# Scoring 64 expert blocks and gathering 36 rows while the PEER gates are laid out

## The chip, the core and the metric

One core of a Trainium2 chip runs the whole program. The metric is device time in microseconds from the first to the last instruction's end. The engines are TensorE (PE, with its weight loads as PEld), VectorE (DVE), ScalarE (ACT), GpSimd (POOL) and SyncE (SP), which here only issues DMAs.

## What is computed

The reference runs two transformer blocks on 512 tokens of width 1024. The change lies in the first block's PEER layer:

```
q      = (hf @ w_query).reshape(t, 8, 256)
s1, s2 = q halves against peer_keys1, peer_keys2         # 128 scores each
v1, i1 = top_k(s1, 16);  v2, i2 = top_k(s2, 16)
sc, ci = top_k(v1[..., :, None] + v2[..., None, :], 16)  # 16 of 256 pairs
idx    = i1 * 128 + i2 of the chosen pairs;  gates = softmax(sc)
a      = gelu(hf . peer_u[idx]);  out = sum(gates * a * peer_v[idx])
```

Each token chooses 8 x 16 = 128 of 16384 experts.

## The kernel before

The 512 tokens are four blocks of 128. Blocks 0 to 2 (384 tokens, `NDT = 3`) are computed **densely**: all 16384 experts, in 128 expert blocks of 128, are scored against them by matrix products, weighted by a gate tensor that is zero where an expert was not chosen, and multiplied by `peer_v`. Block 3 is computed by **gathering**: for each of its 128 choices per token, one indirect DMA fetches a row of `peer_u` (later of `peer_v`) for each of 128 tokens, 512 KB in all.

The float32 products are made of three float32r products (`mm3`): an operand is split into a high part (ACT copies it, `act(hi, raw, AF.Copy)`) and a low part (raw minus high, a TENSOR_TENSOR, L439 for `peer_u`).

The stages of `peer`, in the order of the program:

- `queries(h)` for eight heads: query products, keys, top 16.
- `decode(0)`: a generator that turns block 0's top 16s into expert numbers and gates. It has ten yields. After each one, `early_u(1)` scores one expert block ahead of its turn: load (`uraw`, four buffers), high part (ACT, L438), low part (DVE, L439), 24 matmuls (`aps`, two PSUM buffers), Gelu (ACT, L622), store to DRAM (`Ad`, SP, L623). Which blocks are scored early is set by `AHEAD`: 5 of every 16, that is 40 of 128 (`EARLY`). The tiles `uhi` and `ulo` have two buffers each.
- `spread(t, step)` for t = 0, 1, 2: lays the gates of token block t out as a dense tensor. It has 8 steps, so 24 in all. A step makes one-hot tiles `of` (16 TENSOR_SCALAR, DVE, L601) and `ob` (2, DVE, L605), widens `ob` to `oq` (2, ACT, L606), multiplies them (`gps`, PE, L610), copies the product out (4, ACT, L612) and stores it (2 DMAs on SP, L614). After each step, `step()` runs `early_u(1)` and two yields of `decode(t + 1)`. `decode(3)` ends with `gidx`, the row numbers for the gathers, and `ggate`.
- `early_u(len(EARLY))`: the six early blocks that are left.
- The main loop over the 128 expert blocks, in an order written out by hand (`manual_schedule`): a block that was not scored early is scored (24 matmuls with 384 columns), then weighted, split and multiplied by `peer_v` (18 matmuls with 512 columns into six PSUM accumulators). `pace` puts `gather_step(n)` between them, n = 0 to 255: an indirect DMA (POOL, L652) and its use, for n below 128 a multiply with row sum (L659), then a multiply-add into `gacc` (L665). `row` has five buffers here.

Outside `manual_schedule` the order of each engine's instructions is chosen by the framework's scheduler, which may take an instruction of a later step first when its inputs are ready; each engine then runs its own list strictly in order. The second block of the reference follows and is not touched.

Of the kernel before, what the change touches and what calls it, by code (L numbers as in the profile page):

```python
# [9 lines left out]
F32 = mybir.dt.float32  # L10
# [4 lines left out]
AF = mybir.ActivationFunctionType  # L15
ALU = mybir.AluOpType
# [4 lines left out]
P = 128  # L21
D = 1024
# [3 lines left out]
NEG = -1e30  # L26
LOW = -3e38
NDT = 3
TD = NDT * P
AHEAD = (1, 4, 7, 10, 13)  # L30
MAGIC = 12582912.0
TWO_PI_HI = 6.28125
TWO_PI_LO = 2.0 * math.pi - 6.28125
# [2 lines left out]
def body(ctx, tc, I, O):  # L36
# [355 lines left out]
    with ExitStack() as px:  # L392
        peer(px, tc, I, locals())
# [9 lines left out]
def peer(px, tc, I, E):  # L403
    nc = tc.nc
    mm = nc.tensor.matmul
    act = nc.scalar.activation
    vtt = nc.vector.tensor_tensor
    vts = nc.vector.tensor_scalar
    stt = nc.vector.scalar_tensor_tensor
# [9 lines left out]
    htm = kp.tile([P, D], F32, name="htm", tag="htm")  # L419
    gidx = kp.tile([P, P], I32, name="gidx", tag="gidx")  # L420
    ggate = kp.tile([P, P], F32, name="ggate", tag="ggate")
    e1T = kp.tile([P, TD], F32, name="e1T", tag="e1T")
    e2T = kp.tile([P, TD], BF16, name="e2T", tag="e2T")
    gT = kp.tile([P, TD], F32, name="gT", tag="gT")
    gs2 = kp.tile([P, KD], F32, name="gs2", tag="gs2")
    NBK = TD // 16
    Gd = [drp.tile([P, NBK, 64, 16], F32, name=f"Gd{c}") for c in range(2)]
    up = E["up"]
    papp = px.enter_context(tc.tile_pool(name="papp", bufs=2, space=PSUM))
    EARLY = [e for e in range(P) if e % 16 in AHEAD]  # L430
    Ad = drp.tile([len(EARLY), P, TD], F32, name="Ad")

    def u_split(e, lo_engine):
        raw = up.tile([P, KD, P], F32, name="uraw", tag="uraw", bufs=4)
        nc.sync.dma_start(raw, I["peer_uT"][e])
        hi = up.tile([P, KD, P], F32R, name="uhi", tag="uhi")
        lo = up.tile([P, KD, P], F32R, name="ulo", tag="ulo")
        act(hi, raw, AF.Copy)  # L438
        lo_engine.tensor_tensor(lo, raw, hi.bitcast(F32), op=ALU.subtract)  # L439
        return hi, lo  # L440

    def u_matmuls(hi, lo):
        ps = papp.tile([P, TD], F32, name="aps", tag="aps")
        for k in range(KD):
            mm3(ps, hi[:, k], lo[:, k], hh[:, k, :TD], hl[:, k, :TD], k == 0, k == KD - 1)
        return ps

    with ExitStack() as qx:
        gp = qx.enter_context(tc.tile_pool(name="gp", bufs=2))
        ioj = gp.tile([P, 16, P], BF16, name="ioj", tag="ioj", bufs=1)  # L450
# [45 lines left out]
        def queries(h):  # L496
            qT = []
            for half in range(2):
                if h == 0:
                    ps = ps0[half]  # L500
                else:
                    ps = pp.tile([P, T], F32, name="mmp", tag="mmp")
                    proj_block(ps, wq.get(2 * h + half), (hh, hl))
                q = qp.tile([P, T], F32, name="qT", tag="qT", bufs=4)
                act(q, ps, AF.Copy)
                qT.append(q)
            for t in (3, 0, 1, 2):
                sp = pp.tile([P, 2, P], F32, name="sp", tag="sp", bufs=2)
                for half in range(2):
                    mm(sp[:, half], qT[half][:, t * P:(t + 1) * P], keysT[:, 2 * h + half], start=True, stop=True)  # L510
                s = sq_.tile([P, 2, P], F32, name="s", tag="s", bufs=4)
                act(s, sp, AF.Copy)
                for half in range(2):
                    top16(VVs[:, t, h, half], IIs[:, t, h, half], s[:, half])
# [79 lines left out]
        def spread(t, step):  # L594
            for blk in range(8 * t, 8 * t + 8):
                st = gp.tile([P, P, 16], F32, name="st", tag="st")
                for hb in range(2):
                    c0 = 16 * blk + 8 * hb
                    of = gp.tile([P, 8, P], F32, name="of", tag="of")
                    for j in range(8):  # L600
                        vts(of[:, j], iop, e1T[:, c0 + j:c0 + j + 1], gT[:, c0 + j:c0 + j + 1],  # L601
                            op0=ALU.is_equal, op1=ALU.mult)
                    oq = gp.tile([P, 8, P], F32, name="oq", tag="oq")
                    ob2 = gp.tile([P, P, 8], BF16, name="ob2", tag="ob2")
                    vtt(ob2, iob, e2T[:, None, c0:c0 + 8].to_broadcast([P, P, 8]), op=ALU.is_equal)  # L605
                    act(oq.rearrange("p t e -> p e t"), ob2, AF.Copy)  # L606
                    for t4 in range(2):
                        ps = pp.tile([P, 4, P], F32, name="gps", tag="gps")
                        for j in range(4):
                            mm(ps[:, j], oq[:, 4 * t4 + j], of[:, 4 * t4 + j], start=True, stop=True)  # L610
                        o = 8 * hb + 4 * t4
                        act(st[:, :, o:o + 4], ps.rearrange("p t e -> p e t"), AF.Copy)  # L612
                for c in range(2):
                    nc.sync.dma_start(Gd[c][:, blk], st[:, 64 * c:64 * c + 64])  # L614
                step()

        early = iter(range(len(EARLY)))

        def early_u(count):
            for n in itertools.islice(early, count):  # L620
                gl = up.tile([P, TD], F32, name="gle", tag="gle", bufs=2)
                act(gl, u_matmuls(*u_split(EARLY[n], nc.vector)), AF.Gelu)  # L622
                nc.sync.dma_start(Ad[n], gl)  # L623

        for h in range(8):
            queries(h)
        for _ in decode(0):
            early_u(1)
        for t in range(NDT):
            dec = decode(t + 1)  # L630

            def step():
                early_u(1)
                for _ in itertools.islice(dec, 2):
                    pass

            spread(t, step)
            for _ in dec:
                pass

    early_u(len(EARLY))


    rp = px.enter_context(tc.tile_pool(name="rp", bufs=1))
    outp = rp.tile([P, D], F32, name="gacc", tag="gacc")
    nc.vector.memset(outp, 0.0)
    ga = rp.tile([P, P], F32, name="ga", tag="ga")
    scr = rp.tile([P, D], F32, name="gscr", tag="gscr")

    def gather(src, j):  # L650
        row = rp.tile([P, D], F32, name="row", tag="row", bufs=5)
        nc.gpsimd.indirect_dma_start(out=row, out_offset=None, in_=I[src],  # L652
                                     in_offset=bass.IndirectOffsetOnAxis(ap=gidx[:, j:j + 1], axis=0))
        return row

    def gather_step(n):
        if n < P:
            row = gather("peer_u", n)
            stt(scr, row, 1.0, htm, op0=ALU.mult, op1=ALU.mult, accum_out=ga[:, n:n + 1])  # L659
        else:  # L660
            if n == P:
                act(ga, ga, AF.Gelu)
                vtt(ga, ga, ggate, op=ALU.mult)
            row = gather("peer_v", n - P)
            stt(outp, row, ga[:, n - P:n - P + 1], outp, op0=ALU.mult, op1=ALU.add)  # L665

    ppo = px.enter_context(tc.tile_pool(name="ppo", bufs=1, space=PSUM))
    acc = [[ppo.tile([P, T], F32, name=f"acc{t}{c}", tag=f"acc{t}{c}") for c in range(2)] for t in range(NDT)]
    GG = 8
# [33 lines left out]
    def v_matmuls(e, wh, wl, vh, vl):  # L703
        order = [(t, c) for t in range(NDT) for c in range(2)]
        if e == P - 1:
            order.sort(key=lambda tc_: tc_[1])
        for t, c in order:
            mm3(acc[t][c], wh[:, t * P:(t + 1) * P], wl[:, t * P:(t + 1) * P],
                vh[:, c * T:(c + 1) * T], vl[:, c * T:(c + 1) * T], e == 0, e == P - 1)

    total = 2 * P - len(EARLY) - 4
    done = [0, 0]

    def pace(units):
        done[0] += units
        while done[1] < 2 * P and done[1] * total < done[0] * 2 * P:
            gather_step(done[1])
            done[1] += 1

# [47 lines left out]
    for c in range(2):  # L767
        sts = [rp.tile([P, T], F32, name="ot", tag="row", bufs=5) for t in range(NDT)]
        for t in range(NDT):
            act(sts[t], acc[t][c], AF.Copy)  # L770
# [769 lines left out]
```

## Time and profile before

| | us |
|---|---|
| median of 3 runs (2838.25 to 2846.59) | 2843.0 |
| the profiled execution | 2841.45 |
| its span, first to last instruction | 2839.7 |
| PE busy (12617 matmuls) | 2586.8 (91%) |
| DVE busy | 1445.1 (51%) |
| ACT busy | 915.6 (32%) |
| POOL busy | 451.3 (16%) |

The shares are over the whole span; the stages differ greatly, and the argument is read by stage. A busy time counts overlapping instructions once. Matmuls are pipelined, so one that "lasts" 0.34 us starts about 0.17 us after the one before it: the cost of a run of matmuls is read from their starts.

### The profile page before, as it was taken

How to read it: one execution, taken by the hardware profiler on the slowest of the kernel's cores; microseconds unless marked ns; L12 is line 12 of the kernel's file. 1: busy time of each engine (PE TensorE's matmuls, PEld its weight loads, DVE VectorE, ACT ScalarE, POOL GpSimd, SP SyncE). 2: the span in 40 equal slices, each digit the busy share in tenths (PEclk: the TensorE clock that was granted, in tenths of full speed). 3: DMA queues.
4: the chain of work that ended last, by engine and by line, in shares of the span. 5: the costliest groups of instructions: out<-in, count | busy, mean ns of one | idle time of the engine just before them, and what ended most of it. 6: DMA issues, size and time to landing. Idle time of an engine off the chain costs nothing. (4 is left out here: it accounts for less than half of the span.)

```text
span 2839.7 us, 32851 instructions
## 1 busy us (share of the span) xinstructions
PE 2586.8 (91%) x12617; PEld 1810.0 (64%) x12617; DVE 1445.1 (51%) x2879; ACT 915.6 (32%) x1369; POOL 451.3 (16%) x335
## 2 busy tenths in 40 slices
PE   7998999988999999999999999969888888788887
PEld 5666778988899889988898777633323223232332
DVE  4485899994777877778777655330101101011011
ACT  4463438984333333333333434220000000000001
POOL 0001000000444444344444113010000000000000
PEclk9999999999999999999999999989999999999999
DMA  6344224556889899889988422379999999999997
GB/s 237 121 160 163 75 93 175 212 193 223 306 314 330 310 316 331 317 308 319 321 311 318 155 93 79 123 302 428 428 427 426 429 427 428 428 428 428 427 428 305
DMA packets 195078, 826.41 MB, mean 291 GB/s; under 512 B 17160, under 2 KB 77448, under 8 KB 167145
## 3 DMA queue, kind: packets, MB, share of 16 engines
q1 hardware_dynamic: 154280, 680.67, 61.1%
q0 software_dynamic: 38016, 138.43, 13.7%
q10 hardware_dynamic: 2624, 5.22, 0.5%
q8 instruction: 99, 1.62, 0.2%
q14 instruction: 59, 0.48, 0.1%
HBM read 787.02 MB, written 37.22 MB: 290 GB/s over the span
## 5 line engine op out<-in xcount | busy, mean ns | idle before, releaser
L1349 DVE TENSOR_TENSOR sg<-sg,upp 128x512 f32<-128x512 f32 x32 | 22.0, 688 | 754.7 <-PE upp L1342 754.7
L85 PE MATMUL aps<-hh,uhi 128*128 128x384 f32 x1024 | 348.3, 340 | 7.9 <-ACT gle L622 7.9
L87 PE MATMUL aps<-hh,ulo 128*128 128x384 f32 x1024 | 346.1, 338 | 5.1 <-DVE ulo L439 5.1
L86 PE MATMUL aps<-hl,uhi 128*128 128x384 f32 x1024 | 345.9, 338 | 0.0
L1342 PE MATMUL upp<-wch,XB 128*64 128x512 f32 x1024 | 269.1, 616 | 46.2 <-DMA wch<-in_w_up 46.2
L1342 PE MATMUL gp<-wch,XB 128*64 128x512 f32 x1024 | 273.1, 620 | 37.5 <-DMA wch<-in_w_gate 37.5
L85 PE MATMUL acc<-vh,wh 128*128 128x512 f32 x768 | 300.0, 391 | 2.4 <-ACT wh L81 2.4
L87 PE MATMUL acc<-vh,wl 128*128 128x512 f32 x768 | 300.4, 391 | 0.0
L86 PE MATMUL acc<-vl,wh 128*128 128x512 f32 x768 | 299.9, 390 | 0.3 <-DVE vl L82 0.3
L652 POOL DMA_INDIRECT row<-in_peer_u,gidx x128 | 191.3, 1494 | 633.9 <-issue 386.9
L1368 PE MATMUL y<-wch,aT 128*64 128x512 f32 x1024 | 247.6, 598 | 11.9 <-ACT aT L1354 11.9
L652 POOL DMA_INDIRECT row<-in_peer_v,gidx x128 | 187.1, 1462 | 254.2 <-DVE gacc L665 221.5
L1342 PEld LDWEIGHTS gp<-wch,XB 128*64 128x64 f32 x1024 | 85.3, 142 | 206.3 <-issue 149.4
L1342 PEld LDWEIGHTS upp<-wch,XB 128*64 128x64 f32 x1024 | 84.8, 141 | 204.0 <-issue 138.2
L438 ACT ACTIVATE uhi<-uraw 128x1024 fp32r<-128x1024 f32 x128 | 135.6, 1059 | 235.1 <-DMA uraw<-in_peer_uT 185.0
L439 DVE TENSOR_TENSOR ulo<-uraw,uhi 128x1024 fp32r<-128x1024 f32 x128 | 156.4, 1222 | 106.4 <-ACT uhi L438 105.6
L85 PEld LDWEIGHTS aps<-hh,uhi 128*128 128x128 f32 x1024 | 194.2, 190 | 13.0 <-ACT gle L622 9.5
L87 PEld LDWEIGHTS aps<-hh,ulo 128*128 128x128 f32 x1024 | 193.8, 189 | 6.1 <-DVE ulo L439 6.1
L86 PEld LDWEIGHTS aps<-hl,uhi 128*128 128x128 f32 x1024 | 194.2, 190 | 4.0
L1348 ACT ACTIVATE sg<-gp 128x512 f32<-128x512 f32 x32 | 19.1, 597 | 491.7 <-PE gp L1342 491.7
L1368 PEld LDWEIGHTS y<-wch,aT 128*64 128x64 f32 x1024 | 84.9, 136 | 141.4 <-issue 122.6
L665 DVE SCALAR_TENSOR_TENSOR gacc<-row,ga,gacc 128x1024 f32<-128x1024 f32 x128 | 164.1, 1282 | 2.4
(406 smaller groups left out, 4261.5 us busy)
## 6 DMA issues: line engine op xcount, KB each, us to landing
wch<-in_w_gate SPq DMA_DIRECT2D x64, 2048.0 KB, 35.4
wch<-in_w_up SPq DMA_DIRECT2D x62, 2048.0 KB, 33.0
wch<-in_w_down SPq DMA_DIRECT2D x62, 2048.0 KB, 34.4
uraw<-in_peer_uT SPq DMA_DIRECT2D x128, 512.0 KB, 7.7
vraw<-in_peer_v SPq DMA_DIRECT2D x128, 512.0 KB, 6.6
Gd<-st SPq DMA_DIRECT2D x48, 512.0 KB, 3.6
gg<-Gd SPq DMA_DIRECT2D x16, 1536.0 KB, 16.5
wraw<-in_w_in SPq DMA_DIRECT2D x36, 512.0 KB, 3.2
```

The lines of the kernel that those rows point to most:

```text
L85: mm(out, lh, rh, start=first, stop=False)
L86: mm(out, lh, rl, start=False, stop=False)
L87: mm(out, ll, rh, start=False, stop=last)
L438: act(hi, raw, AF.Copy)
L439: lo_engine.tensor_tensor(lo, raw, hi.bitcast(F32), op=ALU.subtract)
L652: nc.gpsimd.indirect_dma_start(out=row, out_offset=None, in_=I[src], in_offset=bass.IndirectOffsetOnAxis(ap=gidx[:, j:j + 1], axis=0))
L665: stt(outp, row, ga[:, n - P:n - P + 1], outp, op0=ALU.mult, op1=ALU.add)
L1342: mm(ps[64 * e:64 * e + 64], xT[:, k, 64 * e:64 * e + 64], gu[w][e][:, o:o + T], start=k == 0, stop=k == KD - 1)
L1348: act(sg, ps2[0], AF.Silu)
L1349: vtt(sg, sg, ps2[1], op=ALU.mult)
L1368: mm(y[c][64 * e:64 * e + 64], aT[:, fb, 64 * e:64 * e + 64], dn[e][:, o:o + T], start=fc == 0 and fb == 0, stop=fc == 3 and fb == 3)
```

## The change

`AHEAD` names 8 of every 16 blocks in place of 5 (the odd ones), so 64 blocks are scored early. In `decode(0)`'s early blocks, the low part is made on GpSimd. In `spread`, each step scores two blocks in place of one. The decodes of the other three token blocks run in the order 1, 3, 2 in one chain of yields. From the step in which `decode(3)` has ended (the eleventh of 24), each step also uses the two rows gathered one step before and gathers two more, into a pool `gr` with two buffers of its own; after the last step, five rounds of one early block and one such `rows_step` bring the number of rows to `NGE = 36`. One early block is left for the end. The use of a `peer_u` row now writes its product over the row in place of a scratch tile. The main loop starts its gathers at row 36 and spreads the remaining 220 over its length.

```diff
-AHEAD = (1, 4, 7, 10, 13)
+NGE = 36
+AHEAD = (1, 3, 5, 7, 9, 11, 13, 15)
...
+    gr = px.enter_context(tc.tile_pool(name="gr", bufs=1))
+    ga = gr.tile([P, P], F32, name="ga", tag="ga")
+    sums, homes = [], [(gr, 2)]
+
+    def gather(n):
+        pool, bufs = homes[-1]
+        row = pool.tile([P, D], F32, name="row", tag="row", bufs=bufs)
+        j = n % P
+        nc.gpsimd.indirect_dma_start(out=row, out_offset=None, in_=I["peer_u" if n < P else "peer_v"],
+                                     in_offset=bass.IndirectOffsetOnAxis(ap=gidx[:, j:j + 1], axis=0))
+        return row
+
+    def use_row(n, row):
+        if n < P:
+            stt(row, row, 1.0, htm, op0=ALU.mult, op1=ALU.mult, accum_out=ga[:, n:n + 1])
+        else:
...
+    def gather_step(n):
+        use_row(n, gather(n))
...
-        def early_u(count):
+        def early_u(count, sub=nc.vector):
...
-                act(gl, u_matmuls(*u_split(EARLY[n], nc.vector)), AF.Gelu)
+                act(gl, u_matmuls(*u_split(EARLY[n], sub)), AF.Gelu)
...
         for _ in decode(0):
+            early_u(1, nc.gpsimd)
+        ended = []
+
+        def decodes():
+            for t in (1, 3, 2):
+                yield from decode(t)
+                ended.append(t)
+
+        dec = decodes()
+        rows = []
+
+        def rows_step():
+            for n, row in rows:
+                use_row(n, row)
+            n0 = rows[-1][0] + 1 if rows else 0
+            rows[:] = [(n, gather(n)) for n in range(n0, min(n0 + 2, NGE))]
+
+        def step():
+            early_u(2)
+            for _ in itertools.islice(dec, 2):
+                pass
+            if 3 in ended and (not rows or rows[-1][0] + 1 < NGE):
+                rows_step()
+
+        for t in range(NDT):
+            while t and t not in ended:
+                next(dec, None)
+            spread(t, step)
+        while rows:
             early_u(1)
-        for t in range(NDT):
-            dec = decode(t + 1)
-
-            def step():
-                early_u(1)
-                for _ in itertools.islice(dec, 2):
-                    pass
-
-            spread(t, step)
-            for _ in dec:
-                pass
+            rows_step()
...
-    ga = rp.tile([P, P], F32, name="ga", tag="ga")
-    scr = rp.tile([P, D], F32, name="gscr", tag="gscr")
...
+    sums.append(outp)
+    homes.append((rp, 5))
...
-    done = [0, 0]
+    done = [0, NGE]
...
-        while done[1] < 2 * P and done[1] * total < done[0] * 2 * P:
+        while done[1] < 2 * P and (done[1] - NGE) * total < done[0] * (2 * P - NGE):
```

## Rows read from the trace of the kernel before

**Rows 1.** Busy time in four stretches: start:end, length, PE, PEld, DVE, ACT, POOL.

```profile
408.40:452.00 43.60, 36.31 (x195) 34.92 (x196) 42.26 (x193) 24.86 (x29) 0.00 (x0) 0.96 0.38 134
452.00:664.00 212.00, 192.92 (x1326) 184.85 (x1327) 194.37 (x656) 185.99 (x207) 0.00 (x0) 0.98 0.53 196
664.00:705.00 41.00, 35.31 (x193) 34.36 (x191) 11.51 (x11) 13.48 (x19) 5.14 (x5) 0.95 0.72 260
705.00:1580.00 875.00, 874.51 (x4330) 784.12 (x4331) 689.05 (x849) 319.52 (x425) 373.24 (x251) 1.00 0.90 315
```

**Rows 2.** PE's timeline in the main loop: start, us, engine, line, operation.

```profile
1002.67 0.34 PE L85 MATMUL aps<-hh,uhi 128*128 128x384 f32 x1
...
1006.83 0.39 PE L85 MATMUL acc<-vh,wh 128*128 128x512 f32 x1
...
1015.00 0.34 PE L85 MATMUL aps<-hh,uhi 128*128 128x384 f32 x1
```

**Rows 3.** PE's costliest group from 452 to 664 us.

```profile
L610 PE MATMUL gps<-of,oq 128*128 128x128 f32 x768 | 98.3, 282 | 17.7 <-ACT oq L606 9.8 <-ACT st L612 7.9
```

**Rows 4.** PE's waits from 408.4 to 452 us: total us, times, longest.

```profile
PE aps L87 <- DVE ulo L439: 5.1, 3, 2.0
PE aps L85 <- ACT gle L622: 2.2, 2, 1.3
```

**Rows 5.** PE's two largest waits from 452 to 664 us.

```profile
PE gps L610 <- ACT oq L606: 9.8, 10, 1.5
PE gps L610 <- ACT st L612: 7.9, 9, 1.6
```

**Rows 6.** Waits from 664 to 705 us.

```profile
ACT gle L622 <- DMA Ad<-gle: 6.4, 2, 6.1
...
PE aps L85 <- ACT gle L622: 3.4, 1, 3.4
```

**Rows 7.** DVE's costliest groups from 452 to 664 us.

```profile
L601 DVE TENSOR_SCALAR of<-iop,e1T,gT 128x128 f32<-128x128 f32 x384 | 103.8, 344 | 10.5 <-PE gps L610 10.3
L605 DVE TENSOR_TENSOR ob<-iob,e2T 128x1024 bf16<-128x1024 bf16 x48 | 32.5, 687 | 2.9 <-ACT oq L606 2.9
L439 DVE TENSOR_TENSOR ulo<-uraw,uhi 128x1024 fp32r<-128x1024 f32 x24 | 29.3, 1221 | 1.9 <-ACT uhi L438 1.8
```

**Rows 8.** ACT's groups from 452 to 664 us.

```profile
L606 ACT ACTIVATE oq<-ob 128x1024 f32<-128x1024 bf16 x48 | 98.1, 2052 | 8.4 <-DVE ob L605 8.4
...
L438 ACT ACTIVATE uhi<-uraw 128x1024 fp32r<-128x1024 f32 x24 | 25.5, 1061 | 8.6 <-PE aps L86 8.6
L622 ACT ACTIVATE gle<-aps 128x384 f32<-128x384 f32 x23 | 11.1, 483 | 0.0
```

**Rows 9.** The use of a `peer_u` row on DVE, whole span.

```profile
L659 DVE SCALAR_TENSOR_TENSOR gscr<-row,htm 128x1024 f32<-128x1024 f32 x128 | 156.4, 1222 | 2.3
...
L659 DVE DVE_READ_ACCUMULATOR gscr<-row,htm 128x1 f32 x128 | 10.6, 83 | 0.0
```

**Rows 10.** A TENSOR_TENSOR of 128x1024 on POOL, by form.

```profile
L478 POOL TENSOR_TENSOR hg<-hh,hl 128x1024 f32<-128x1024 f32 x1 | 2.4, 2389 | 23.1 <-DVE hl L169 23.1
```

**Rows 11.** DVE's timeline, 243 to 272 us.

```profile
243.11 1.21 DVE L219 SCALAR_TENSOR_TENSOR wada<-wada,c 128x1024 f32<-128x1024 f32 x1
...
244.25 2.30 DVE L219 SCALAR_TENSOR_TENSOR wada<-wada,c 128x1024 f32<-128x1024 f32 x1
```

**Rows 12.** POOL's timeline in the same stretch.

```profile
244.01 1.47 POOL L386 TENSOR_TENSOR sx<-sx,sq 128x512 f32<-128x512 f32 x1 [1.36 <-ACT sq L133]
```

**Rows 13.** POOL's timeline, 660 to 760 us: two gathers of the first five.

```profile
671.16 1.12 POOL L652 DMA_INDIRECT row<-in_peer_u,gidx  x1 [366.79 <-issue]
672.59 0.93 POOL L652 DMA_INDIRECT row<-in_peer_u,gidx  x1 [0.30 <-issue]
```

**Rows 14.** DMA issue to landing of all 256 gathers, by source line.

```profile
DMA to landing us min/median/max: 4.9/8.0/11.2
```

**Rows 15.** The same of the five gathers issued from 660 to 680 us.

```profile
DMA to landing us min/median/max: 9.4/9.8/10.1
```

**Rows 16.** ACT's timeline, 380 to 460 us: decode(1)'s widening and the first `oq`.

```profile
442.31 1.91 ACT L560 ACTIVATE wb__3862<-d 128x2048 bf16<-128x2048 f32 x1
...
455.59 2.07 ACT L606 ACTIVATE oq<-ob 128x1024 f32<-128x1024 bf16 x1 [3.38 <-DVE ob L605]
```

**Rows 17.** DMA traffic from 705 to 1580 us.

```profile
DMA packets 118808, 275.30 MB, mean 315 GB/s; under 512 B 8288, under 2 KB 59360, under 8 KB 118752
```

More of the change, by code (lines that the diff above doesn't have):

```diff
@@ L446, in u_matmuls @@
         return ps
+    gr = px.enter_context(tc.tile_pool(name="gr", bufs=1))
[12 more added lines that the diff above has]
+        else:
+            if n == P:
+                act(ga, ga, AF.Gelu)
+                vtt(ga, ga, ggate, op=ALU.mult)
+            stt(sums[0], row, ga[:, n - P:n - P + 1], sums[0], op0=ALU.mult, op1=ALU.add)
+    def gather_step(n):
+        use_row(n, gather(n))
     with ExitStack() as qx:
@@ L646, in peer @@
     nc.vector.memset(outp, 0.0)
-    ga = rp.tile([P, P], F32, name="ga", tag="ga")
-    scr = rp.tile([P, D], F32, name="gscr", tag="gscr")
[L650 to L665, printed above, removed]
+    sums.append(outp)
+    homes.append((rp, 5))
     ppo = px.enter_context(tc.tile_pool(name="ppo", bufs=1, space=PSUM))
```

## The prediction

> **What bounds the kernel now.** I first read busy time by stretch, because the whole-span shares mix stages with different limits. From 705 to 1580 us, the main loop, PE is busy 874.5 of 875 us, DVE 689 and ACT 320 [rows 1]: PE bounds it, and nothing else comes near. From 452 to 664 us, while the gates are laid out, three engines are each busy some nine tenths: PE 192.9, DVE 194.4 and ACT 186.0 of 212 us. From 408.4 to 452 us (decode of token block 0) DVE is busy 42.3 of 43.6 us, PE 36.3. From 664 to 705 us PE finishes the early blocks, 35.3 of 41.0 us.
>
> Next I read PE's own timeline, for what one block really costs. The 24 matmuls of a scored block start at 1002.67 and the next group at 1006.83: **4.16 us a block**. The 36 matmuls after them, two blocks' products with `peer_v`, run from 1006.83 to 1015.00, 4.08 us a block [rows 2].
>
> Last come the waits. PE's idle time from 408.4 to 705 us is 7.3 + 19.1 + 5.7 = **32.1 us** of 296.6 [rows 1]. In the first part 5.1 us of it are waits for the low part from DVE, 2.2 us for a Gelu that frees a PSUM tile [rows 4]. In the second, 9.8 us are waits for `oq` and 7.9 us for the copy `st`, both on ACT [rows 5]. In the third, 3.4 us follow a Gelu that itself waited 6.1 us for a store to `Ad` [rows 6].
>
> **The identity behind the sum.** The change moves PE work and removes none: 24 blocks leave the main loop (24 x 4.16 = 99.8 us) and enter the stretch before it. Where PE is always busy, the main loop gives back those 99.8 us; the stretch before it must take in the same 99.8 us. So the result is the change in PE's idle time before the main loop, and the most that can be won there is 32.1 us.
>
> **The main loop.** It falls from 875 to 775 us if PE still bounds it. DVE loses 24 low parts (1.22 us each [rows 7]) and 36 row uses (1.222 + 0.083 = 1.305 us [rows 9]): 689 - 29.3 - 47.0 = 613 us, 79% of 775, as it was 79% of 875. DMA loses 24 loads and 36 gathers of 0.524 MB (128x1024 float32) and gains 24 loads of 0.197 MB from `Ad`: 275.3 - 31.5 + 4.7 = 248.5 MB, or 321 GB/s against 315 now [rows 17]. No engine's share rises, so I price this at -99.8 us. ACT's 24 high parts and Gelus leave too, at nothing, since PE covers them; POOL's 36 gathers likewise.
>
> **Decode of block 0.** The ten low parts go to POOL, idle until then [rows 1]. The nearest row, a 128x1024 TENSOR_TENSOR on POOL, took 2.389 us [rows 10], less than the 4.16 us that PE needs for the block, so PE is fed in time and the 5.1 us of waits go; DVE sheds 10 x 1.22 = 12.2 us. Idle there: 7.3 - 5.1 = 2.2 us. Against this speaks what a DVE instruction with two inputs in SBUF does beside a POOL tensor operation: the same SCALAR_TENSOR_TENSOR took 1.21 us alone and 2.30 us [rows 11] when it started 0.24 us after one on POOL of 1.47 us [rows 12]. I price that below, as a rival. The Trainium skill, SBUF — State Buffer, section Who interferes with whom, says why: the two engines share one pair of ports under an exclusive lock, and a DVE instruction with two SBUF inputs waits out a GpSimd instruction that reads SBUF; the trace agrees, by those 1.09 us. By that rule alone, this part of the change would win nothing.
>
> **The gate layout.** PE's work becomes 98.3 (`gps` [rows 3]) + 48 x 4.16 = 298 us. DVE: 194.4, plus 24 low parts, 29.3, plus 14 steps of two row uses, 36.5: 260 us. (Of DVE's 194.4 now, `of`, `ob` and the low parts are 103.8 + 32.5 + 29.3 [rows 7]; the two decodes that fall here are the other 28.8.) ACT: 186 + 24 x (1.061 + 0.483) [rows 8] = 223 us. In some 306 us that is PE 97%, DVE 85%, ACT 73%, where it was 91, 92 and 88. PE waited for ACT, and ACT is relieved most; each step has also twice as many scoring matmuls to put between the `gps` bursts. Of the idle 19.1 us the 17.7 behind ACT can fall to nothing, or stay in proportion (rival 2); I take a bit under half of the whole, **8 us**, as ACT's idle share (12% to 27%) more than doubles.
>
> The moved issues: SP gets 24 loads of `uraw` and 24 stores to `Ad` more in this stretch, and a load queues behind a store that waits for its Gelu. I cost this at nothing, since four `uraw` buffers reach two steps ahead; without that cover a step would wait one Gelu, about 0.5 us [rows 8]. POOL's queue holds only gathers by then: a gather waits for the DVE use that frees its buffer, and nothing but the next gather stands behind it.
>
> **The added wait** is DVE's: a row use waits for its gather to land, and behind it on DVE stand the next step's `of`, `ob` and low parts, and behind those ACT and PE. A gather was issued 1.4 us after the one before it [rows 13] and landed after 8.0 us in the median, 4.9 to 11.2 [rows 14]: the second row of a pair is there 9.4 us after the first issue, and a step lasts 306/24 = 12.8 us. In the program's order the row is there in time; even at 11.2 us it is 0.2 us early. So I price the wait at nothing in the steps.
>
> **The end of the layout.** Ten rows (26 to 35) are still unused when the steps end, in five rounds, beside six blocks or 25 us for PE. One round can't be shorter than issue, landing and use of one buffer: 1.25 (half the way between the 1.1 us that a gather lasted and the 1.4 between two) + 8.0 + 1.3 = 10.6 us, five of them 53 us. But the scheduler takes instructions early when an engine is free: `decode(1)`, written into the first steps, was at 442 us already in its last part, before the first `oq` at 455.6 [rows 16]. With DVE free 15% of the layout I expect the rows to run some two rounds ahead, so that 53 becomes about 32 against 25, of which I count **8 us** idle in this part, in place of 5.7.
>
> **Sum.** Idle 2.2 + 8 + 8 = 18 in place of 32.1: -14 us. The profiled execution took 2841.45 us, 1.55 below the median of 2843.0; -14 on the median gives **2829 us**. A measurement of this kernel can tell about 0.3%, 8.5 us, from no change.
>
> **Rivals.**
>
> 1. *The rows hold DVE at the end of the layout* (slower). If the rows keep the program's order, the five rounds last 53 us, PE has 25 us of work beside them, and the main loop's first low parts stand behind the last row use on DVE: 28 us idle more, in place of the 2 counted, -14 + 26 = +12, 2855 us. With the landing of 9.8 us that the first five gathers show, issued beside other loads [rows 15], it is 62 us and +21, 2864. It decides as soon as fewer than two rounds are ahead when the last step ends. For it: 23 Gelus of scored blocks fall into the 24 steps [rows 8], so those did not run ahead of the program, and two buffers allow no more than one pair in flight. Against it: DVE's free time. Chance 0.27.
> 2. *The three lines stay as tightly coupled as now* (slower). If PE idles in the same proportion, 32.1/264.5 = 12.1% of 264.5 + 99.8, that is 44.2 us: +12, 2855 us. For it: two buffers in every tile of the step. Against it: DVE's and ACT's shares fall. Chance 0.10.
> 3. *The lock eats the relief in the first decode* (no change). By the code a decode has 22 DVE instructions with two SBUF inputs, and two decodes ran there [rows 16]. POOL is busy 10 x 2.39 = 24 of 43.6 us, so about 24 of the 44 meet it; at 1.09 us each [rows 11] that is 26 us, less 12.2 shed: the stretch grows by 14 us, PE has no more blocks for it, and -14 becomes 0: 2843 us. Against it: both may find gaps, and the second decode need not run there. Chance 0.10.
> 4. *PE never waits before the main loop*: -32, 2811 us. Chance 0.07.
>
> **Chances.** My forecast, between -6 and -25 us, has 0.46; about a seventh of that is within 0.3%. Faster: 0.46 x 0.85 + 0.07 = 0.46. Within 0.3%: 0.07 + 0.10 and a little of rivals 1 and 2: 0.21. Slower: 0.33. Both signs hold weight; the forecast's own range is 2818 to 2837. The range of 8 in 10 reaches from rival 4 to rival 1 at the slow landing: 2811 to 2864.
>
> **What the changed profile would show.** A main loop some 775 us long with PE as busy in it as now (if it is longer, the -99.8 fails). In the first decode no waits of PE for the low part; DVE's two-input operations as long as before (if they double, rival 3). In the layout, steps of 12.5 to 13 us and PE's waits for `oq` and `st` under 8 us (if near 20 or more, rival 2). At its end, row uses done within about 10 us of the last scored block; a gap on PE of 20 us or more, with DVE waiting for `row`, is rival 1. DVE waiting for `row` inside the steps would show the one-step distance too short, and make the prediction wrong altogether.

## The result, and the profile after

The changed kernel takes **2868.0 us** (median of 5 runs, 2857.01 to 2871.29) against 2843.0: slower, ratio 1.0074, 95% interval 1.0052 to 1.0096 (the two medians alone give 1.0088). The forecast was 2829, within 2811 to 2864; the sign is wrong and the median lies outside the range. The profiled execution spans 2866.2 us, 26.5 more than before.

The same four stretches as in [rows 1], here cut at marks that both kernels have (first candidate sum of the decode, first `of`, end of the last copy `st`, first and last matmul into `acc`). In the kernel after:

```profile
core 0: us, PE busy (x) PEld busy (x) DVE busy (x) ACT busy (x) POOL busy (x), PEclk, DMA share, GB/s
406.30:457.90 51.60, 40.15 (x200) 38.19 (x199) 51.02 (x222) 25.01 (x30) 17.57 (x7) 0.83 0.36 122
457.90:767.20 309.30, 288.65 (x1871) 282.00 (x1870) 255.93 (x718) 220.29 (x252) 50.07 (x36) 0.98 0.71 249
767.20:810.60 43.40, 39.14 (x216) 38.50 (x214) 11.76 (x11) 14.24 (x21) 5.66 (x5) 0.96 0.69 252
810.60:1617.60 807.00, 793.52 (x3814) 696.07 (x3815) 620.68 (x760) 290.38 (x386) 318.64 (x215) 0.99 0.89 308
```

Length minus PE's busy time is PE's idle time: 11.45, 20.65, 4.26 and 13.5 us. With the same marks in both kernels, and the forecast's terms beside them:

| us | before | forecast | after |
|---|---|---|---|
| PE idle in the first decode | 7.5 | 2.2 | 11.5 |
| PE idle in the layout | 19.1 | 8 | 20.7 |
| PE idle at its end | 5.3 | 8 | 4.3 |
| PE busy in these three | 264.5 | 264.5 + 99.8 = 364.3 | 367.9 |
| main loop, first to last `acc` matmul | 888.0 | 888.0 - 99.8 = 788.2 | 807.0 |
| rest of the span, ahead and behind | 1655.3 | 1655.3 | 1654.9 |

The forecast missed by 18.4 us of idle time ahead of the main loop (36.4 for 18), by 3.6 us of busy time there, and by 18.8 us in the main loop: 40.8 us in all. -14 + 40.8 = +26.8, and the spans differ by 26.5. So there are two failures of about one size, one on each side of the mark at 810.6 us.

**First decode.** PE has traded its waits: in place of those for the low part from DVE [rows 4] it now waits behind the decode itself, the low part on POOL, and the high part.

```profile
PE pt L612 <- DVE ee L597: 4.3, 1, 4.3
PE aps L88 <- POOL ulo L440: 3.7, 2, 2.3
PE aps L86 <- ACT uhi L439: 3.4, 2, 2.8
```

DVE's groups there by form (total busy us, mean ns, idle us before): the candidate sums took 284 ns before, and others with two inputs are longer too:

```profile
L545 DVE TENSOR_TENSOR cand<-VVs 128x128 f32<-128x128 f32 x3 | 5.0, 1659 | 0.0
...
L596 DVE TENSOR_TENSOR oh<-oh 128x512 bf16<-128x512 bf16 x4 | 3.7, 914 | 0.0
...
L610 DVE TENSOR_TENSOR g<-g,gden 128x128 f32<-128x128 f32 x2 | 2.7, 1369 | 0.0
```

**Layout.** Waits of the stretch 457.9 to 767.2 us (total, times, longest). The waits of [rows 5] have shrunk from 9.8 and 7.9 to 4.2 and 2.8 us, as forecast. In their place stands a new pair: DVE waits for a gathered row, and PE for a low part.

```profile
DVE row L463 <- DMA row<-in_peer_u,gidx: 34.9, 13, 6.1
...
PE aps L88 <- DVE ulo L440: 13.6, 4, 4.8
...
PE gps L635 <- ACT oq L631: 4.2, 5, 0.9
...
PE gps L635 <- ACT st L637: 2.8, 2, 1.8
```

The pair in DVE's timeline: a row is awaited for 6.05 us, the next for 1.36, and the low part comes behind both.

```profile
662.90 1.22 DVE L463 SCALAR_TENSOR_TENSOR row<-row,htm 128x1024 f32<-128x1024 f32 x1
...
670.18 1.23 DVE L463 SCALAR_TENSOR_TENSOR row<-row,htm 128x1024 f32<-128x1024 f32 x1 [6.05 <-DMA row<-in_peer_u,gidx]
...
672.78 1.22 DVE L463 SCALAR_TENSOR_TENSOR row<-row,htm 128x1024 f32<-128x1024 f32 x1 [1.36 <-DMA row<-in_peer_u,gidx]
...
673.93 1.22 DVE L440 TENSOR_TENSOR ulo<-uraw,uhi 128x1024 fp32r<-128x1024 f32 x1
```

POOL's timeline has the gather that was awaited, issued 8.06 us before its use could start; PE's has the end of its own wait:

```profile
662.12 1.68 POOL L457 DMA_INDIRECT row<-in_peer_u,gidx  x1 [4.76 <-DVE row L463]
```

```profile
675.20 0.44 PE L88 MATMUL aps<-hh,ulo 128*128 128x384 f32 x1 [4.79 <-DVE ulo L440]
```

The forecast's spacing, a step of 12.8 us between gather and use, is not in this timeline: these rows are used as soon as they land. The view by tile shows how far ahead of the program the uses run:

```profile
L463 DVE SCALAR_TENSOR_TENSOR row<-row,htm x36: 1204/1219/1227, 535.3 to 731.6; 128x1024 f32<-128x1024 f32 x36
```

In the program's order the first use belongs to the 12th of 24 steps, some 600 us (457.9 + 11 x 309.3/24), and the last ten rows come after the last step. The first use is at 535.3 and the last at 731.6, 35 us before the layout ends.

**Main loop.** Before, ACT waited there for `uraw` too, but PE's two waits for `wh` were of 2.4 us in all, 1.9 of them at the loop's opening (704 to 1592 us):

```profile
ACT uhi L438 <- DMA uraw<-in_peer_uT: 185.0, 68, 7.5
```

Now (waits from 810.6 to 1617.6 us):

```profile
ACT uhi L439 <- DMA uraw<-in_peer_uT: 97.9, 37, 7.9
...
PE acc L86 <- ACT wh L82: 14.9, 9, 3.7
```

One of the nine, on three timelines. SP issues the load late, behind a `vraw` load that waits for its buffer:

```profile
1045.27 5.45 SPq L704 DMA_DIRECT2D vraw<-in_peer_v  x2
1050.78 0.42 SPq L707 DMA_DIRECT2D gl<-Ad  x1
1051.25 0.42 SPq L436 DMA_DIRECT2D uraw<-in_peer_uT  x1
```

ACT is free 5 us later, waits 7.92 us for it, and the next block's `vh`, `gl` and `wh` stand behind:

```profile
1064.42 1.06 ACT L439 ACTIVATE uhi<-uraw 128x1024 fp32r<-128x1024 f32 x1 [7.92 <-DMA uraw<-in_peer_uT]
1065.39 1.04 ACT L82 ACTIVATE vh<-vraw 128x1024 fp32r<-128x1024 f32 x1
1066.34 0.47 ACT L767 ACTIVATE gl<-aps 128x384 f32<-128x384 f32 x1
1068.38 0.52 ACT L82 ACTIVATE wh<-w 128x384 fp32r<-128x384 f32 x1 [1.57 <-DVE w L719]
```

PE stands for 3.72 us and then starts a matmul every 0.43 us, where the same matmuls of [rows 2] started every 8.17/36 = 0.227 us:

```profile
1068.95 0.79 PE L86 MATMUL acc<-vh,wh 128*128 128x512 f32 x1 [3.72 <-ACT wh L82]
...
1070.40 0.63 PE L86 MATMUL acc<-vh,wh 128*128 128x512 f32 x1
1070.82 0.63 PE L87 MATMUL acc<-vl,wh 128*128 128x512 f32 x1
```

Three theories went into the experiments. **A**: the lock between POOL and DVE in the first decode (the prediction's rival 3) costs the stretch before the main loop some of its time. **B**: in the layout DVE, running in order, waits for rows brought forward, and PE behind it; the rival is that the late second decode, or simply more work, fills that stretch. **C**: the main loop loses because each load from `peer_u` is issued too late, behind a short step (an early block's, without scoring); the rival is that DMA has become the bound. The time from a load's issue until ACT is free for it is called its lead below.

### The profile page after: what moved, and what is told of

Its sections match the earlier page's. It is cut to its first block, busy times and chain, and to the rows that moved or that the text cites. A ratio compares the mean times of both kernels' runs of the same rounds, so it can differ in the third digit from the quotient of the medians.

```text
span 2866.2 us, 33004 instructions
## 1 busy us (share of the span) xinstructions
PE 2596.0 (91%) x12617; PEld 1817.5 (63%) x12617; DVE 1437.6 (50%) x2869; ACT 916.4 (32%) x1369; POOL 472.2 (16%) x345
## 3 DMA queue, kind: packets, MB, share of 16 engines
q0 software_dynamic: 38016, 138.43, 13.6%
## 5 line engine op out<-in xcount | busy, mean ns | idle before, releaser
L88 PE MATMUL aps<-hh,ulo 128*128 128x384 f32 x1024 | 347.9, 340 | 17.3 <-DVE ulo L440 13.6
L1368 PE MATMUL upp<-wch,XB 128*64 128x512 f32 x1024 | 275.0, 626 | 52.8 <-DMA wch<-in_w_up 52.8
L86 PE MATMUL acc<-vh,wh 128*128 128x512 f32 x768 | 302.3, 394 | 15.1 <-ACT wh L82 14.9
L1368 PE MATMUL gp<-wch,XB 128*64 128x512 f32 x1024 | 266.3, 605 | 31.1 <-DMA wch<-in_w_gate 31.0
L457 POOL DMA_INDIRECT row<-in_peer_u,gidx x128 | 184.9, 1444 | 500.2 <-DVE row L463 360.3
L440 DVE TENSOR_TENSOR ulo<-uraw,uhi 128x1024 fp32r<-128x1024 f32 x118 | 144.0, 1221 | 106.8 <-ACT uhi L439 102.7
L86 PEld LDWEIGHTS acc<-vh,wh 128*128 128x128 f32 x768 | 145.2, 189 | 46.6 <-ACT wh L82 19.5
L1374 ACT ACTIVATE sg<-gp 128x512 f32<-128x512 f32 x32 | 19.1, 597 | 480.1 <-PE gp L1368 480.1
```

The costliest lines, as they stand in the source:

```text
L86: mm(out, lh, rh, start=first, stop=False)
L88: mm(out, ll, rh, start=False, stop=last)
L1368: mm(ps[64 * e:64 * e + 64], xT[:, k, 64 * e:64 * e + 64], gu[w][e][:, o:o + T], start=k == 0, stop=k == KD - 1)
L1374: act(sg, ps2[0], AF.Silu)
```

## The experiments

Eleven kernels. All ratios are to the kernel before, measured beside it; "to the loop" is the time from the first candidate sum to the first `acc` matmul. The stretches are of one profiled execution each, which lies within 3 us of the kernel's median (e8 4 us below it, e10 6 and e11 5 above). Before and e8 have the same program up to the main loop and differ by 4.3 us there, by 1.4 in the layout: smaller differences say nothing.

| kernel | first decode | layout | end | to the loop | main loop | median | ratio, 95% |
|---|---|---|---|---|---|---|---|
| before | 45.2 | 211.1 | 40.1 | 296.4 | 888.0 | 2843.0 | |
| after | 51.6 | 309.3 | 43.4 | 404.3 | 807.0 | 2868.0 | 1.0052 to 1.0096 |
| e1 | 43.7 | 317.7 | 42.9 | 404.3 | 807.6 | 2868.3 | 1.0070 to 1.0106 |
| e2 | 51.6 | 287.9 | 42.1 | 381.6 | 847.9 | 2889.5 | 1.0143 to 1.0188 |
| e3 | 51.7 | 308.5 | 41.3 | 401.5 | 786.8 | 2844.1 | 0.9993 to 1.0014 |
| e4 | 51.5 | 303.2 | 42.9 | 397.6 | 805.0 | 2858.6 | 1.0034 to 1.0072 |
| e5 | 43.7 | 303.2 | 41.6 | 388.5 | 786.6 | 2832.9 | 0.9953 to 0.9979 |
| e6 | 51.7 | 287.9 | 41.4 | 381.0 | 786.9 | 2822.1 | 0.9909 to 0.9951 |
| e9 | 52.2 | 305.3 | 41.7 | 399.2 | 786.8 | 2839.9 | 0.9979 to 1.0005 |
| e7 | 51.6 | 292.4 | 40.8 | 384.8 | 786.6 | 2828.0 | 0.9933 to 0.9966 |
| e8 | 43.8 | 209.7 | 38.6 | 292.1 | 887.0 | 2838.3 | 0.9971 to 0.9992 |
| e10 | 43.8 | 291.3 | 45.2 | 380.3 | 788.9 | 2821.6 | 0.9901 to 0.9934 |
| e11 | 52.1 | 308.7 | 44.1 | 404.9 | 793.1 | 2849.9 | 1.0012 to 1.0036 |

### e1: the first decode's low parts back on DVE

```diff
         for _ in decode(0):
-            early_u(1, nc.gpsimd)
+            early_u(1)
```

> The first decode's low parts go back to DVE, all else as in the changed kernel. From the first candidate sum to the first one-hot tile of the layout it took 45.2 us before and 51.6 after. Theory A (DVE's two-input operations wait out GpSimd's low parts): the stretch falls to about 45 us, the 128x128 candidate sums last 0.28 us each again and not up to 2.37, and the whole is 6 to 12 us faster than the changed kernel. Rival (DVE is simply full there and GpSimd relieves it by 12 us): the stretch grows to 55 us or more and the whole gets 5 us slower.

The first decode falls from 51.6 to 43.7 us, the layout grows by 8.4, and the median does not move (2868.3 for 2868.0). The candidate sums last 0.28 us again, as A expected, but what A expected of the whole is refuted. DVE's groups show the exchange. In after, five instructions there were held by the lock, 2.33 to 2.45 us each in place of 0.21 to 0.42, 10.5 us more in all; seven low parts, 8.5 us, are gone from DVE in exchange; and 32 small instructions of the next decode (222 instructions for 197, with seven low parts less) fall into the longer stretch, which the layout is then spared (718 for 751). Up to the main loop DVE is busy 51.0 + 255.9 + 11.8 = 318.7 us in after and 43.7 + 261.6 + 11.7 = 317.0 in e1: the lock took what the move gave. PE's idle time went the same way: 5.5 us less in the first decode (5.9 for 11.5), 7.4 more in the layout (28.1 for 20.7), where its waits for the low part grew from 13.6 us to

```profile
PE aps L88 <- DVE ulo L440: 18.3, 7, 10.1
```

Why the layout gives back just as much is not shown.

### e2: no rows beside the layout

```diff
-NGE = 36
+NGE = 0
```

> No row is gathered in the layout (the main loop takes all 256), all else as in the changed kernel. Theory B (row uses wait for their gathers at the head of DVE's list, and the low part behind them starves PE at the border between the second and third layout): the hole there (PE busy 29.7 of 40 us from 640 to 680) closes by most of its 10 us and by the slow clock after it, and the layout is 10 to 18 us shorter; the main loop gets longer by what 36 more gathers cost it, 0 if PE bounds it as before, up to 30 if DMA or DVE does. Rival (the hole is the late decode of token block 2, whatever the rows do): the layout is shorter by less than 4 us.

The layout falls by 21.4 us to 287.9, and PE's wait for the low part, 13.6 us in after, is gone: B. The decode of token block 2 still ends late there (its `e1T`, from which the one-hot tiles are made, came at 655.7 us, some 7 us past two thirds of the layout, as in after), so its lateness alone is not the cause. All 256 gathers now lie in the main loop, and that grows by 41 us, more than the layout gave. PE's waits from 787.3 to 1635.2 us in it:

```profile
ACT uhi L439 <- DMA uraw<-in_peer_uT: 123.6, 36, 7.6
...
PE acc L86 <- ACT wh L82: 40.2, 16, 4.8
```

The same wait as in after, but 40.2 us of it. By itself this fits C and its rival alike: e3 and e6 separate them.

### e3: loads from `peer_u` one scored block earlier in the main loop

```diff
     def prepare(i):
+        for j in (i, i + 1):
+            if j < len(late) and j not in raws:
+                raws[j] = u_load(late[j])
         if i < len(late):
-            usp[late[i]] = u_split(late[i], nc.vector)
+            usp[late[i]] = u_split(late[i], nc.vector, raws[i])
```

(`u_load` is the first two lines of `u_split`; nothing but the place of the load in SP's queue changes.)

> In the main loop each block of peer_u is loaded one scored block earlier, all else as in the changed kernel. Theory C (with every second block scored early, each load of peer_u is issued only one short step before ACT needs it; where the gate load falls together with it ACT waits up to 8 us and holds the other splits, and PE stands, then runs at the lower clock): ACT's waits for peer_u in the main loop fall from 98 us to under 30, PE's waits for the weighted tile from 14.9 to 3 us, the main loop from 807 to about 788 us, the whole 15 to 20 us faster than the changed kernel. Rival (DMA is simply full there): the waits move to other loads and the main loop stays above 800 us.

The main loop, in the window from its first to its last matmul:

```profile
805.70:1592.50 786.80, 786.44 (x3813) 695.40 (x3814) 621.75 (x760) 288.83 (x386) 342.95 (x215) 1.00 0.91 315
```

786.8 us, 1.4 less than the 788.2 forecast, PE busy all of it, clock 1.00. ACT no longer waits for `uraw` at all, PE for `wh` only the 1.9 us of the opening. The median falls by 24 us, 4 more than expected. The bytes are the same and go at 315 GB/s in place of 308, so DMA was not the bound: C.

### e4: three parts of a decode a step

```diff
-            for _ in itertools.islice(dec, 2):
+            for _ in itertools.islice(dec, 3):
```

> Three yields of the decodes a step in place of two, so that token block 2 is decoded by step 11 of 16 and rows start at about step 7; all else as in the changed kernel. Theory D (the border hole comes from the decode of token block 2 ending with the very last step before its layout): the hole closes, the layout is 10 to 15 us shorter. Theory B: row uses still wait inside the steps, and as the rows start earlier and end in the layout the hole is moved, not closed: less than 5 us.

The decode of token block 2 gave its `e1T` at 599.0 us in place of 670.9. The layout falls by 6.1 us, between what D and B expected, and DVE's wait for rows from 34.9 to 29.1. A late second decode is a small part of the loss; that it acts through the rows is likely from those 5.8 us, not shown.

### e5: e1, e3 and e4 together

> Earlier loads of peer_u, three yields of the decodes a step, and the first decode's low parts on DVE, with 36 rows. If the single effects add up (24, 9 and 0 us), the whole is some 33 us faster than the changed kernel, 2835 us, and 8 us faster than the kernel before. If the layout's gain with three yields came from rows that had only moved, it stays at 2844 us.

2832.9 us, 2 below the 2835 of adding up: the medians add up within their spread. Ahead of the main loop the edits of e1 and e4 give 13 us here (401.5 to 388.5) though alone they gave 0 and 6.7.

### e6: e3, and no rows beside the layout

> The earlier loads of peer_u, and no row gathered in the layout: the main loop takes all 256. Theory C (the loop's loss was the late load of peer_u alone): the main loop, 847.9 us without rows and with late loads, falls to about 790 us, the layout stays at 288 us, and the whole is 15 to 20 us faster than the changed kernel with earlier loads alone, so faster than the kernel before. Rival (256 gathers in a loop shorter by 100 us fill DMA, 339 GB/s against 315): the main loop stays above 810 us and the whole gains nothing.

```profile
404.50:456.20 51.70, 40.20 (x201) 38.25 (x201) 51.10 (x223) 25.06 (x30) 17.65 (x7) 0.83 0.37 122
456.20:744.10 287.90, 281.71 (x1870) 276.18 (x1869) 215.89 (x646) 219.90 (x252) 0.00 (x0) 1.00 0.56 202
744.10:785.50 41.40, 37.53 (x215) 36.89 (x213) 11.67 (x11) 14.31 (x21) 5.59 (x5) 1.00 0.75 279
785.50:1572.40 786.90, 786.52 (x3813) 695.57 (x3814) 661.28 (x832) 289.17 (x386) 390.34 (x251) 1.00 0.95 339
```

2822.1 us, faster than both kernels, and 22 below e3 (15 to 20 expected). All 256 gathers fit under 786.9 us, at 339 GB/s and a DMA share of 0.95, with the same loop length as e3 has with 220. So once the loads come earlier, moving rows out of the main loop buys nothing there, and costs the layout 20.6 us (308.5 to 287.9). This also closes C's rival: e2, with the same traffic and late loads, took 847.9.

### e9 and e7: 26 rows, as the scheduler places them, and held to the program's order

e9 is e3 with `NGE = 26`, the rows whose uses fall into the steps. e7 is e9 with the uses queued behind the last low part written before them:

```diff
+    lows = []
...
-        lo_engine.tensor_tensor(lo, raw, hi.bitcast(F32), op=ALU.subtract)
+        lows.append(lo_engine.tensor_tensor(lo, raw, hi.bitcast(F32), op=ALU.subtract))
...
-            for n, row in rows:
-                use_row(n, row)
+            with tc.issue_after(lows[-1].ins):
+                for n, row in rows:
+                    use_row(n, row)
```

> The earlier loads of peer_u, and 26 rows in place of 36 in the layout, placed by the scheduler. Theory B (each pair of rows costs DVE a wait for its landing): the layout is between 288 us (no rows) and 308 us (36 rows), the waits of DVE for rows fall from 33 us in proportion to the rows or more.

> As with 26 rows, but each use of a row is queued on DVE behind the second low part of its own step, so that the scheduler cannot bring it forward. Theory B with its cause (the scheduler brings the uses some five steps forward, which makes the one step between gather and use a few us): DVE waits for rows less than 5 us in all, PE's waits for the low part in the layout vanish, and the layout is 5 to 15 us shorter than with 26 rows placed freely. Rival (two row buffers are too few for the landing, wherever the use stands): the waits for rows stay above 15 us.

The waits of the layout in e9, where DVE's for rows fall a little less than in proportion to the rows (33.0 x 26/36 = 23.8):

```profile
DVE row L467 <- DMA row<-in_peer_u,gidx: 25.3, 9, 6.1
PE aps L88 <- DVE ulo L444: 10.5, 5, 3.5
```

and in e7, where those two lines do not occur; PE's waits there are

```profile
PE gps L641 <- ACT oq L637: 4.6, 5, 1.3
...
PE gps L641 <- ACT st L643: 3.0, 3, 1.1
...
PE aps L86 <- ACT gle L653: 1.1, 1, 1.1
```

The same 26 rows cost 305.3 us of layout in one order and 292.4 in the other; without rows it is 287.9. So of the rows' price 12.9 us is the order, and 4.5 us what is left with 26 uses held in place. The distance of one step is enough when it is kept. The last ten rows in the program's order, the subject of rival 1, were not run.

### e8: the earlier load in the kernel before

The edit of e3, in the kernel before.

> The kernel before, with each load from peer_u in the main loop issued one scored block earlier, and nothing else. If the late load is a loss that the change itself brought in (PE waited for nothing in the main loop of before: busy 874.5 of 875 us), the earlier load has nothing to give back here: main loop 887 to 888 us, median 2841 to 2845. Rival: the earlier load speeds up any main loop of this kind, and e3's 24 us are no loss of the change; then the main loop is 10 to 20 us shorter and the median 2823 to 2833.

```profile
696.10:1583.10 887.00, 886.65 (x4389) 795.27 (x4390) 697.04 (x856) 326.19 (x434) 410.76 (x251) 1.00 0.88 310
```

ACT's waits for `uraw` (185.0 us, 68 times, before) are gone, and the main loop is 1.0 us shorter. The median, 5 us below the 2843.2 measured beside it, is 3 below the band expected; the difference does not lie in the main loop. So the loss that e3 repairs was brought in by the change.

### e10: e6 with the edits of e1 and e4

> e6 (no rows beside the layout, loads from peer_u earlier) with the first decode's low parts back on DVE and three parts of a decode a step. With rows, these two edits together gave 13 us before the main loop (401.5 to 388.5), though the low parts on DVE alone gave nothing, since the layout then waited longer behind the rows. If rows were what took the shorter first decode back, it stays won here: first decode 44 us, layout 283 to 288, from the candidate sums to the main loop 368 to 374 us, main loop 787, median 2809 to 2815. Rival: the early part is bound by PE and DVE whatever the order, and the layout takes the 8 us again: 381 us, 2820 to 2824.

The rival's number is right: median 2821.6, 380.3 us to the loop for 381.0. The first decode is 7.9 us shorter and the layout and its end 7.2 longer, without a row there to wait for, so rows are not what takes the shorter decode back. DVE is busy 278.0 us up to the loop, 278.7 in e6. But 3.8 of the 7.2 us lie in the end, where PE ran at a clock of 0.92 (1.00 in e6), and this execution is the slowest of e10's six, so what takes the decode's gain back stays open. With e6 this is the fastest kernel of the study, and the two can't be told apart.

### e11: early blocks in pairs

```diff
-AHEAD = (1, 3, 5, 7, 9, 11, 13, 15)
+AHEAD = (2, 3, 6, 7, 10, 11, 14, 15)
```

> The kernel after, with the 64 early blocks in pairs (two scored in the main loop, then two early) in place of every second one; 36 rows, loads issued as in after. A load's lead is the step before its own: 4.1 us behind an early block, 8.2 us behind a scored one. If that lead is what the main loop of after lost, only 32 of the 64 loads are short here, fewer than the 40 that before had without a wait of PE: main loop 787 to 797 us, median 2846 to 2858. Rival: the number of loads and gathers in a shorter main loop is the cause, whatever the order: 805 to 809 us, median 2866 to 2870.

The main loop is 793.1 us and the median 18 us below after, with loads, rows and their number unchanged; only the order of scored and early blocks differs. (One scored block more lies ahead of the first `acc` matmul, 3792 matmuls for 3814, so in like terms it is some 797.) PE waits 6.3 us in place of 14.9, in seven waits of at most 1.7:

```profile
PE acc L86 <- ACT wh L82: 6.3, 7, 1.7
```

This is C by another road: the leads are 7.7 us behind a scored block and 4.8 behind an early one (medians), and about half of the loop's loss goes. It also shows that the number of loads behind an early block does not decide by itself: 32 of them cost some 9 us here, 40 cost nothing before.

## Why the prediction was wrong

**The main loop: the step that failed is "No engine's share rises, so I price this at -99.8 us".** The shares came out as forecast (DVE 620.7 us for 613, 308 GB/s for 321), and PE still lost 18.8 us. What decided was a load that comes late and what PE has left to do meanwhile. SP reaches a block's `uraw` load 6.3 us before ACT is free for it (median; 1.7 to 8.1), since the `vraw` load ahead of it waits for DVE, and it lands after 7.1 us in the median, 14.5 at most. Neither is worse than before (lead 6.9, 0.5 to 11.6; landing 8.8, at most 13.1). ACT's wait was on view there, 68 times, and the prediction did not read that row; but it cost PE no more than 0.5 us. Seven of its eight waits above 5 us fell where three scored blocks follow one another, as the one shown here, with PE busy all of the 8 us:

```profile
1250.88 1.06 ACT L438 ACTIVATE uhi<-uraw 128x1024 fp32r<-128x1024 f32 x1 [7.50 <-DMA uraw<-in_peer_uT]
```

```profile
1244.00:1252.00 8.00, 8.00 (x42) 7.34 (x41) 3.76 (x4) 1.11 (x2) 3.81 (x3) 1.00 1.05 393
```

With every second block early, the block behind each scored one needs no scoring, so while ACT stands, with the next block's operands behind it, PE has one product of 4.08 us to run. ACT's five waits above 5 us came through to PE less some 4.3 us each: 7.9 as 3.7, 7.5 as 3.2, 5.9 as 1.6, 5.6 as 1.3, 5.2 as 0.9. The long waits belong to the 1.5 MB `gg` loads, one every eight blocks: of PE's waits behind the opening one, seven of eight begin 24.6 to 27.4 us after such a load was issued, and in e2 14 of 15 (24.8 to 27.6 us). e3 shows that the late load is the cause, e8 that it cost the kernel before nothing, and e11 that the order of scored and early blocks matters at equal traffic. That the order acts by PE's shorter cover is read from these waits; no run changes the cover alone.

**The layout: the step that failed is "In the program's order the row is there in time ... So I price the wait at nothing in the steps".** The number behind it holds: held to the program's order (e7) the rows are never awaited, PE's idle time in the layout is 8.7 us where 8 were forecast, and the stretch to the loop takes 384.8 us where the forecast's terms make 364.3 + 18 = 382.3. But the scheduler does not keep that order, and the prediction knew it: in the next paragraph it lets rows run two rounds ahead, as a relief for the end. It used the freedom where it helped and not where it hurts. A use that is taken early sits in DVE's list at a place where its row has not landed, and everything behind it waits: 34.9 us on DVE, 13.6 on PE. The prediction had named this sign, DVE waiting for `row` inside the steps, but read it as a distance too short, where it was the order. The other half of the argument stood: PE's waits for `oq` and `st` fell from 17.7 to 7.0 us, so rival 2 is out. (DVE's sum there counts 14 steps of row uses, and by the program 13 have them, 26 rows: 2.6 us too many, of no consequence.)

**The end of the layout** came out better than forecast, 4.3 us for 8; the rows were done by then. Rival 1 named the right mechanism, rows holding DVE, at the wrong place.

**The first decode: the step that failed is "PE is fed in time and the 5.1 us of waits go".** Rival 3 was right about it: the relief is eaten, and PE's idle time there went from 7.5 to 11.5 us. Its size was off: it counted 24 instructions at 1.09 us [rows 11], and five were caught, at 2.1 us each. The Trainium skill, SBUF — State Buffer, section Who interferes with whom, says that the port pair which the two engines share is an exclusive lock, and that a DVE instruction with two SBUF inputs contends for it with a GpSimd instruction that reads SBUF. The trace agrees, as these two, 0.28 us each when alone, last until a low part on POOL ends (its row holds two, one behind the other):

```profile
423.06 2.33 DVE L545 TENSOR_TENSOR cand<-VVs 128x128 f32<-128x128 f32 x1
425.31 2.45 DVE L610 TENSOR_TENSOR g<-g,gden 128x128 f32<-128x128 f32 x1
```

beside, in POOL's timeline,

```profile
422.86 4.75 POOL L440 TENSOR_TENSOR ulo<-uraw,uhi 128x1024 fp32r<-128x1024 f32 x2 [10.22 <-ACT uhi L439]
```

The rival's conclusion, that this part is worth nothing in the whole, is what e1's median shows, and e10's beside e6's agrees.

**The identity** (the result is the change in PE's idle time before the main loop) did not hold: that idle time grew by 4.5 us (31.9 to 36.4), the span by 26.5. It assumed a main loop without waits and a busy time that does not change. The same matmuls took 3.6 us more ahead of the loop and 7 more in it (793.5 for 786.4 in e3): some 3 us in the loop at the lower clock behind its longest wait (last section), and some 0.4 us at each other wait, where the first matmuls start further apart.

With the failed steps of the main loop and the layout mended (e7: earlier loads, rows in the program's order) the kernel takes 2828.0 us, where the forecast was 2829; that it agrees so closely is partly chance, since e7 uses 26 rows and still has the longer first decode. Without rows it is 2822.1.

## What to carry to other kernels

Where long and short steps alternate, a bound read from shares does not say whether each step is fed: take the shortest step, and compare the slowest landing, not the median, with the load's lead plus the work that is queued meanwhile. A consumer of a transfer, put in an in-order engine's list by a scheduler, is priced at the earliest place the scheduler may choose, not at its place in the program; if the distance matters, pin it and measure both. And before work is moved out of a loop to relieve it, check that the loop is short of what the work uses: here all 256 gathers fitted under it, once the loads from `peer_u` came earlier.

## What was unexpected of the hardware

A stall of PE can cost more than itself. The granted clock around the wait shown above (window, PE busy, ..., clock):

```profile
1065.00:1069.00 4.00, 0.28 (x3) 0.05 (x1) 2.90 (x4) 2.43 (x5) 0.00 (x0) 0.88 0.07 22
1069.00:1073.00 4.00, 4.00 (x10) 3.13 (x11) 4.00 (x8) 0.85 (x1) 1.79 (x2) 0.50 0.82 297
1073.00:1077.00 4.00, 4.00 (x17) 3.40 (x16) 3.35 (x6) 2.30 (x3) 2.81 (x2) 0.76 0.76 259
1077.00:1085.00 8.00, 8.00 (x41) 7.18 (x40) 5.59 (x8) 1.84 (x4) 1.68 (x1) 1.00 0.91 324
```

After 3.72 us of standing, PE ran at the lower level (0.50 of full speed, 1.2 GHz) until about 1075. Some 14 matmuls at 0.43 in place of 0.227 us are 2.8 us, three quarters of the wait again. In the layout the hole around 670 us did the same: from 664 to 675 the clock was 0.79, from 675 to 680 it was 0.66. Not every wait does it: behind the one of 3.19 us that ended at 1015.2 the clock stayed at 1.00 (PE busy 3.83 us from 1015 to 1019). A forecast in terms of PE's idle time should allow for it as a risk.
